# Splitting the first weights of a mixed-attention kernel on ScalarE and GpSimd instead of ScalarE and VectorE

## The chip, the cores and the metric

The kernel runs on one core of a Trainium2 chip. A core has TensorE (PE: matmuls, with PEld for its weight loads), VectorE (DVE), ScalarE (ACT) and GpSimd (POOL), and SyncE (SP), whose queue issues the kernel's DMA transfers. The metric is the device time of one execution in microseconds (us). The kernel before takes 3007.47 us, the median of three runs (2999.73 to 3012.67).

## What is computed

Two layers work on 2048 tokens of width 1024. Each layer projects its input with one wide matrix, runs four kinds of attention with four heads each (softmax with a forget gate, "fox"; stick-breaking, "sb"; low-rank latent, "mla"; attention to a memory of 256 rows, "mem"), multiplies by a gate, projects back and normalises. Cut to what matters:

```
h_res = layer_norm(x, ln_in_g, ln_in_b)
for l in range(2):
    proj = h_res @ w_in[l]
    fq, fk, fv, f_logit, sq, sk, sv, c_q, c_kv, k_rot, mq, gate = split(proj)
    out_fox = causal softmax attention(fq, fk, fv, forget(f_logit))
    out_sb = stick-breaking attention(sq, sk, sv)
    out_mla = causal softmax attention(from c_q, c_kv, k_rot)
    out_mem = softmax attention(mq, memory)
    y = (concat(out_fox, out_sb, out_mla, out_mem) * silu(gate)) @ w_out[l]
    h_res = layer_norm(alpha * h_res + y)
```

## The kernel before

All values are f32, and TensorE is fed with pairs of f16 numbers: a high half and a low half that holds what the high half left over. A product is three matmuls, high x high, high x low and low x high (`mm3`, lines 271 to 278; the three have the lines 276, 277 and 278). So each weight is read as f32 into a raw tile (pool `rawp`, 5 buffers, line 69), its largest magnitude is found on VectorE (line 128), a power of two `s` that brings it into the range of f16 is worked out (`allmax`, lines 130 to 143, two small matmuls in lines 137 and 142; `pow2`, lines 116 to 122), and then `split` (lines 145 to 147) writes the two halves: ScalarE writes `hi`, the scaled source cast to f16 (line 146), and VectorE writes `lo`, the scaled source minus `hi` (line 147).

The callers of `split` are `wprep` (line 152; the general path for weights, with loads in line 165 and splits in lines 188 and 193), `latent_w` (line 474; the weights of the latent projection: query and key latents, rotary keys and forget logits, 420 columns in all), `mla_up` and `out_proj`. In `latent_w` of the first layer the first `wprep` covers 256 columns (8 splits, each of 256 elements a partition), the second 128 columns (4 such splits), and the loop of lines 506 and 507 splits the remaining 36 columns (4 splits of 72 elements a partition). The call stands in line 1042, behind the first part of the input normalisation and ahead of the first layer.

The start of the program is thus: the input is loaded tile by tile (line 1029), normalised (`layer_norm`, lines 243 to 261: statistics on VectorE in lines 251 to 253, the square root on ScalarE in line 215, its correction on GpSimd in lines 218 to 221, the two passes of the normalisation in lines 256 and 261 on VectorE, or for every second tile in lines 258 on ScalarE and 259 on GpSimd), split into halves (`to_T`, lines 263 to 268: ScalarE in line 266, GpSimd in line 267) and turned by a DMA transpose (line 268) into `hT`. The latent projection (`latent`, lines 539 to 605) multiplies `hT` with the latent weights into a PSUM tile `pl`; for the first chunk of 512 tokens in the first layer it does so in two column ranges, 0 to 256 and 256 to 420 (line 549). The list `PLAN` (line 45) gives the order of the stages of a layer: the latents, then fox, mla, sb and mem in pairs of heads, each in four chunks of 512 tokens; the output projection (line 951) closes a layer.

The order of the instructions on each engine isn't that of the text: the program is laid out ahead of time by a scheduler that follows the order of the text as a priority and its own estimates of time (line 1083), and each engine and each DMA queue then runs its list in order.

Of the kernel before, what the change touches and what calls it, by code (L numbers as in the profile page):

```python
# [13 lines left out]
AF = mybir.ActivationFunctionType  # L14
ALU = mybir.AluOpType
# [34 lines left out]
def hybrid_kernel(ctx: ExitStack, tc: tile.TileContext, x, mem, ln_in_g, ln_in_b, mem_ln_g, mem_ln_b,  # L50
# [7 lines left out]
    def pool(name, bufs, space=None):  # L58
        if space is None:
            return ctx.enter_context(tc.tile_pool(name=name, bufs=bufs))  # L60
        return ctx.enter_context(tc.tile_pool(name=name, bufs=bufs, space=space))
# [13 lines left out]
    op = pool("op", 1)  # L75
# [8 lines left out]
    V, A, G, T = nc.vector, nc.scalar, nc.gpsimd, nc.tensor  # L84
# [57 lines left out]
        T.matmul(ps[:, P:P + n], ones_bf[0:n, :], d[0:n, 0:n], start=True, stop=True)  # L142
        return ps[:, P:P + n]

    def split(hi, lo, src, s, eng=0):
        A.activation(hi, src, AF.Copy, scale=s)
        V.scalar_tensor_tensor(lo, src, s, hi, op0=ALU.mult, op1=ALU.subtract)  # L147

# [3 lines left out]
    def wprep(groups, extra=None):  # L152
# [26 lines left out]
        for g, (srcs, dst) in enumerate(groups):  # L179
            res, s = [], ss[:, g:g + 1]  # L180
            for j in range(len(srcs)):
                if dst is None:
                    w = wp.tile([P, 2, KC, P], F16, name=nm("w"), tag="w")
                    res.append(w)
                for a in range(2):
                    rv = raws[g][2 * j + a].rearrange("p (k n) -> p k n", n=P)
                    if dst is None:
                        split(w[:, 0, a * 4:a * 4 + 4], w[:, 1, a * 4:a * 4 + 4], rv, s)
                    else:
                        his, los = dst(j, 0, a), dst(j, 1, a)  # L190
                        c = 4 // len(his)
                        for i in range(len(his)):
                            split(his[i], los[i], rv[:, i * c:(i + 1) * c], s)
            out.append((res, s, us[:, g:g + 1]))
# [105 lines left out]
    def mem_prologue():  # L300
        at = sc_at[0]
        gb, s, u = load_gb(mem_ln_g, mem_ln_b)
        sc_at[0] = at
        V.tensor_copy(mem_su[0], s)
        V.tensor_copy(mem_su[1], u)
        mt2 = ptp.tile([P, 2, KC, MEM], F16, name=nm("memT"), tag="pt")
        for t in range(2):
            xt = granule("mx")
            dma(xt, mem[t * P:(t + 1) * P])
            layer_norm([xt], gb)  # L310
            to_T(xt, mt2[:, :, :, t * P:(t + 1) * P], True)
        dma(memTd, mt2)
# [161 lines left out]
    def latent_w(l, s_h, u_h):  # L474
# [31 lines left out]
        for k in range(0, KC, 2):  # L506
            split(wl[k, 0][:, :, 384:420], wl[k, 1][:, :, 384:420], rawt[:, k:k + 2], s4)
# [12 lines left out]
    def layer(l, hT, s_h, u_h, ah, latw, norm):  # L520
# [451 lines left out]
        def start(gi):  # L972

            gens = [latent() if g == "lat" else pair(g[:-1], int(g[-1])) for g in PLAN[gi]]
            final = gi == len(PLAN) - 1
            if final:
                next(proj)
            for g in gens:
                next(g)
            return gens  # L980

        coming = start(0)
        for gi in range(len(PLAN)):
            gens, coming = coming, None
            for c in range(NCH):
                if norm:
                    next(norm, None)
                if c == AHEAD[gi] and gi + 1 < len(PLAN):
                    coming = start(gi + 1)
                for g in gens:  # L990
                    next(g)
            if gi + 1 < len(PLAN) and coming is None:
                coming = start(gi + 1)
            if l == 0 and gi == MEM_AT:
                mem_prologue()
# [41 lines left out]
    for l in range(DEPTH):  # L1037
        sc_at[0] = 32
        norm = input_norm() if l == 0 else None
        if norm:  # L1040
            next(norm)
            latw = latent_w(l, s_h, u_h)
        r = layer(l, hT, s_h, u_h, ah, latw, norm)
        if r is not None:
            hT, s_h, u_h, ah, latw = r
# [42 lines left out]
```

## Time and profile before

| | |
|---|---|
| three runs | 3012.67, 3007.47, 2999.73 us |
| profiled execution | 2999.77 us, of which the span from the first to the last instruction is 2998.0 us |
| mean granted clock of TensorE | 0.929 of full speed |
| busy: PE, DVE, ACT, POOL | 2518.7, 1979.8, 1930.7, 1530.0 us |

Busy time is the time in which an engine executes an instruction, not the time in which it waits for one. A row of a timeline gives the start in us from the span's start, the duration in us (of a run of equal instructions, from the first's start to the last's end), the engine, the line of the kernel, the operation, the tiles written and read with their shapes, and the count. Behind it stands in brackets how long the engine was idle before it, and what it waited for.

### The profile page before, as it was taken

The page shows a single profiled execution, that of the slowest core. Times are in us where ns is not written, and L with a number is a line of the kernel's source. Part 1 is how long each engine was busy: PE and PEld are TensorE (multiplying, and loading weights), DVE is VectorE, ACT ScalarE, POOL GpSimd, SP SyncE. Part 2 cuts the span into 40 slices and gives each one's busy share as a digit, 9 for nine tenths or more (in the row PEclk, how much of TensorE's full clock was granted, in tenths as well). Part 3 has the DMA queues.
Part 4 walks back from the last instruction along what each step waited for, and adds up shares of the span by engine and source line. Part 5 has one row for each costly group of instructions (what it writes and reads, how often), then busy time and mean ns, then how long its engine had stood idle before and what let it go on. Part 6 is the DMA issues. An engine that isn't in the chain of part 4 may idle for free. (4 is left out here: it accounts for less than half of the span.)

```text
span 2998.0 us, 47307 instructions
## 1 busy us (share of the span) xinstructions
PE 2518.7 (84%) x16412; PEld 1351.6 (45%) x16412; DVE 1979.8 (66%) x4313; ACT 1930.7 (64%) x3737; POOL 1530.0 (51%) x1079
## 2 busy tenths in 40 slices
PE   3689897888897876998997989888889879669998
PEld 2345454444454542543454545444445435335443
DVE  8946656876657677467545474668674776855665
ACT  3557668887777788573234566587777868776600
POOL 3415555656577889342110355355656868783300
PEclk8899999999998987999998999999999889779999
DMA  7757989998857657668744587798888576575752
GB/s 209 206 125 169 198 164 205 189 186 174 162 108 155 130 117 134 142 150 208 205 125 111 107 175 156 147 205 174 171 167 152 108 160 114 120 158 126 190 176 89
DMA packets 1225039, 469.47 MB, mean 157 GB/s; under 512 B 1040304, under 2 KB 1184944, under 8 KB 1224656
## 3 DMA queue, kind: packets, MB, share of 16 engines
q1 hardware_dynamic: 1224800, 466.46, 71.5%
q8 instruction: 128, 2.10, 0.3%
q14 instruction: 111, 0.91, 0.1%
HBM read 141.07 MB, written 50.53 MB: 64 GB/s over the span
## 5 line engine op out<-in xcount | busy, mean ns | idle before, releaser
L390 POOL TENSOR_TENSOR hl<-sb,hl 128x1024 f16<-128x1024 f32 (+7 forms) x384 | 609.0, 1597 | 648.9 <-ACT hl L389 458.6
L332 PE MATMUL s<-k,q 128*128 128x512 f16 (+3 forms) x1920 | 530.5, 376 | 210.6 <-DVE kp L405 103.9
L871 PE MATMUL o<-pt,v 128*128 128x256 f16 (+3 forms) x3456 | 403.8, 286 | 95.4 <-DMA pt<-hl 94.5
L382 ACT ACTIVATE sb<-sb,sm,sc_all 128x1024 f32<-128x1024 f32 (+7 forms) x384 | 376.4, 982 | 71.7 <-DVE sm L378 71.5
L389 ACT CAST hl<-sb 128x1024 f16<-128x1024 f32 (+7 forms) x384 | 298.3, 791 | 192.7 <-DMA pt<-hl 182.0
L871 PEld LDWEIGHTS <-v 128*64 128x64 f16 (+1 forms) x3456 | 236.4, 108 | 287.5 <-issue 148.7
L332 PEld LDWEIGHTS <-q 128*128 128x128 f16 x1920 | 182.2, 103 | 379.2 <-issue 256.8
L951 PE MATMUL s<-wo,gc 128*128 128x512 f16 x1536 | 338.0, 382 | 5.8 <-DVE yt L955 5.4
L408 POOL TENSOR_TENSOR sg<-sg,kp 128x127 f32<-128x127 f32 (+3 forms) x192 | 283.1, 1480 | 111.8 <-DVE kp L405 90.0
L415 POOL TENSOR_TENSOR hl<-sg,hl 128x128 f16<-128x128 f32 (+3 forms) x192 | 304.2, 1592 | 34.8 <-ACT hl L414 34.4
L369 DVE CUSTOM_DVE_ANT_0 sb<-s,fb 128x512 f32<-128x512 f32 (+2 forms) x320 | 183.7, 606 | 113.1 <-DMA fb<-fds 33.8
L951 PEld LDWEIGHTS <-gc 128*128 128x128 f16 x1536 | 151.2, 99 | 189.3 <-issue 12.6
L371 DVE TENSOR_SCALAR_CACHE_REDUCE sb<-s 128x512 f32<-128x512 f32 (+2 forms) x320 | 185.3, 605 | 67.7 <-POOL hl L390 37.3
L401 ACT ACTIVATE kp<-s,sc_all 128x512 f32<-128x512 f32 (+2 forms) x320 | 198.5, 631 | 41.4 <-PE s L332 28.7
L405 DVE TENSOR_TENSOR_SCAN kp<-kp,s 128x384 f32<-128x384 f32 (+7 forms) x128 | 172.4, 1348 | 79.5 <-ACT sg L402 68.3
L414 ACT CAST hl<-sg 128x128 f16<-128x128 f32 (+3 forms) x192 | 153.3, 803 | 101.1 <-DMA pt<-hl 99.3
L276 PE MATMUL pg<-hT,w 128*128 128x512 f16 x512 | 196.3, 383 | 3.7 <-DVE sb L371 1.5
L402 ACT ACTIVATE sg<-s,sc_all 128x512 f32<-128x512 f32 (+2 forms) x320 | 197.0, 632 | 2.4 <-POOL sg L408 1.8
L278 PE MATMUL pg<-hT,w 128*128 128x512 f16 x512 | 195.9, 383 | 0.3 <-DVE w L147 0.3
L277 PE MATMUL pg<-hT,w 128*128 128x512 f16 x512 | 196.1, 383 | 0.0
L276 PEld LDWEIGHTS <-w 128*128 128x128 f16 x1264 | 125.8, 100 | 149.2 <-issue 12.0
L277 PEld LDWEIGHTS <-w 128*128 128x128 f16 x1264 | 125.6, 99 | 148.0 <-issue 26.2
(238 smaller groups left out, 5712.0 us busy)
## 6 DMA issues: line engine op xcount, KB each, us to landing
raw<-in_w_in_dram SPq DMA_DIRECT2D x100, 256.0 KB, 4.7
q<-q SPq DMA_DIRECT2D x128, 128.0 KB, 2.5
fb<-fds SPq DMA_DIRECT2D x32, 512.0 KB, 4.0
gd<-gh SPq DMA_DIRECT2D x128, 128.0 KB, 2.8
raw<-in_w_out_dram SPq DMA_DIRECT2D x64, 256.0 KB, 3.3
gc<-gd SPq DMA_DIRECT2D x64, 256.0 KB, 4.1
yt<-ah SPq DMA_DIRECT2D x32, 512.0 KB, 6.6
raw<-ctd SPq DMA_DIRECT2D x48, 256.0 KB, 2.8
```

The costliest lines, as they stand in the source:

```text
L276: T.matmul(ps, lh, rh, start=(first and k == 0), stop=False)
L277: T.matmul(ps, lh, rl, start=False, stop=False)
L332: T.matmul(ps[:, :m], qs[:, h, v, j * P:(j + 1) * P], ks[c][:, h, :m], start=(v == 0), stop=last)
L382: A.activation(t, t, AF.Exp, scale=sc, bias=sm[:, j, 2:3], accum_out=su[:, b, col + j:col + j + 1])
L389: A.copy(hi, t)
L390: G.tensor_tensor(lo, t, hi, op=ALU.subtract)
L401: A.activation(keep[:, o:o + m], ps[:, :m], AF.Sigmoid, scale=nsc)
L402: A.activation(w[:, o:o + m], ps[:, :m], AF.Sigmoid, scale=sc)
L408: G.tensor_tensor(w[:, :n - 1], w[:, :n - 1], keep[:, 1:n], op=ALU.mult)
L415: G.tensor_tensor(lo, w, hi, op=ALU.subtract)
L871: T.matmul(o[r0:r1, oc + j0 * P:oc + 256], vs[k // 4][:, k % 4, h, 0:r1 - r0], pcol(pt, a, k % 8, kb, j0), start=(n == 1), stop=(n == total))
L951: T.matmul(ps, gc[a][k // 4][:, k % 4, t * P:(t + 1) * P], wo[k][:, b2, n * 512:(n + 1) * 512], start=(k == 0 and a == 0 and b2 == 0), sto ...
```

## The change

`split` gets a second form, which holds while a flag is set. The flag is set from the start of the program and is cleared in the layer function, right after the first stage of the first layer has been set up. In this form ScalarE scales the raw tile in place, ScalarE copies it into `hi` as f16, and GpSimd subtracts `hi` from the scaled tile into `lo`. VectorE has no part in it. The argument `eng`, which nothing used, is dropped.

```diff
-    def split(hi, lo, src, s, eng=0):
+    first = [True]
+
+    def split(hi, lo, src, s):
+
+        if first[0]:
+            A.activation(src, src, AF.Copy, scale=s)
+            A.copy(hi, src)
+            G.tensor_tensor(lo, src, hi, op=ALU.subtract)
+            return
         A.activation(hi, src, AF.Copy, scale=s)
         V.scalar_tensor_tensor(lo, src, s, hi, op0=ALU.mult, op1=ALU.subtract)
...
         coming = start(0)
+        first[0] = False
         for gi in range(len(PLAN)):
```

## Rows read from the trace of the kernel before

**Rows 1.** The page, part 1: busy time, share of the span, instructions.

```profile
PE 2518.7 (84%) x16412; PEld 1351.6 (45%) x16412; DVE 1979.8 (66%) x4313; ACT 1930.7 (64%) x3737; POOL 1530.0 (51%) x1079
```

**Rows 2.** Line 147, 25 to 70 us: ns min/median/max, starts, forms.

```profile
L147 DVE SCALAR_TENSOR_TENSOR w<-raw,sc_all,w x16: 290/472/2339, 28.9 to 65.0; 128x256 f16<-128x256 f32 x12, 128x72 f16<-128x72 f32 x4
```

**Rows 3.** Stretches: length, busy PE, PEld, DVE, ACT, POOL, clock, DMA.

```profile
0.00:225.00 225.00, 137.60 (x919) 82.37 (x920) 166.64 (x341) 107.78 (x217) 69.59 (x69) 0.90 0.69 180
...
75.00:90.00 15.00, 11.39 (x58) 5.76 (x56) 14.96 (x29) 8.00 (x14) 8.78 (x8) 0.89 0.49 116
```

**Rows 4.** Timeline of ScalarE: the splits' high halves, and a cast of the input.

```profile
28.31 3.30 ACT L146 ACTIVATE w<-raw,sc_all 128x256 f16<-128x256 f32 x8 [0.96 <-DVE sc_all L119]
...
38.66 1.99 ACT L266 CAST hl<-xt 128x1024 f16<-128x1024 f32 x2 [3.93 <-DVE xt L261]
...
62.08 2.68 ACT L146 ACTIVATE w<-raw,sc_all 128x256 f16<-128x256 f32 x8 [5.76 <-DVE sc_all L119]
...
97.06 2.56 ACT L146 ACTIVATE w<-raw,sc_all 128x512 f16<-128x512 f32 x4 [0.65 <-DVE sc_all L119]
```

**Rows 5.** Timeline of VectorE: the splits' low halves and steps around them.

```profile
28.86 5.17 DVE L147 SCALAR_TENSOR_TENSOR w<-raw,sc_all,w 128x256 f16<-128x256 f32 x7
33.95 1.27 DVE L251 BATCH_NORM_STATS2 bst<-xt 128x6 f32<-128x512 f32 x2
35.15 2.29 DVE L147 SCALAR_TENSOR_TENSOR w<-raw,sc_all,w 128x256 f16<-128x256 f32 x1
37.35 1.27 DVE L261 SCALAR_TENSOR_TENSOR xt<-xt,mv,gb 128x1024 f32<-128x1024 f32 x1
...
42.91 2.08 DVE L253 TENSOR_SCALAR mv<-mv 128x2 f32<-128x2 f32 x1
...
61.88 0.16 DVE L119 TENSOR_SCALAR sc_all<-pm 128x2 int32<-128x2 int32 x1 [4.70 <-PE pm L142]
...
62.77 2.48 DVE L147 SCALAR_TENSOR_TENSOR w<-raw,sc_all,w 128x256 f16<-128x256 f32 x8
...
68.64 0.69 DVE L128 TENSOR_REDUCE wm<-raw 128x1 f32<-128x512 f32 x1 [1.24 <-DMA raw<-in_w_in_dram]
...
69.31 0.16 DVE L253 TENSOR_SCALAR mv<-mv 128x2 f32<-128x2 f32 x1
```

**Rows 6.** Timeline of GpSimd beside the two batches.

```profile
32.12 0.37 POOL L221 TENSOR_TENSOR mv<-rt,ry 128x2 f32<-128x2 f32 x1
34.81 2.34 POOL L259 TENSOR_TENSOR xt<-xt,gb 128x1024 f32<-128x1024 f32 x1 [2.31 <-ACT xt L258]
39.78 5.18 POOL L267 TENSOR_TENSOR hl<-xt,hl 128x1024 f16<-128x1024 f32 x2 [2.63 <-ACT hl L266]
...
71.40 0.20 POOL L218 TENSOR_TENSOR rt<-ry,mv 128x2 f32<-128x2 f32 x1 [16.26 <-DVE ry L216]
```

**Rows 7.** GpSimd's groups by form: count, busy us, mean ns, idle.

```profile
L464 POOL TENSOR_TENSOR gh<-og,gh 128x256 f16<-128x256 f32 x128 | 90.7, 709 | 97.2 <-ACT gh L463 97.0
...
L390 POOL TENSOR_TENSOR hl<-sb,hl 128x128 f16<-128x128 f32 x32 | 15.9, 497 | 199.9 <-DVE sm L378 118.3 <-ACT hl L389 79.2 <-issue 1.5
```

**Rows 8.** Timeline of TensorE: three starts after waits.

```profile
47.66 0.40 PE L276 MATMUL pl<-w,hT 128*128 128x256 f16 x1 [6.46 <-DMA hT<-hl]
...
56.35 0.27 PE L137 MATMUL pm<-id_bf,am 128*2 128x128 bf16 x1 [4.15 <-DVE am L135]
...
64.08 0.44 PE L276 MATMUL pl<-w,hT 128*128 128x164 f16 x4 [2.23 <-ACT w L146]
```

**Rows 9.** Waits of SyncE's queue from 14 to 75 us: total, times, longest.

```profile
SPq L165 <- DVE w L147: 4.0, 3, 2.9
```

**Rows 10.** Busy time from the first scores on, first and second layer.

```profile
225.00:1345.50 1120.50, 952.38 (x6547) 522.40 (x6547) 757.59 (x1685) 847.75 (x1622) 704.24 (x487) 0.93 0.78 159
1658.80:2832.00 1173.20, 990.00 (x6795) 540.31 (x6795) 765.91 (x1669) 852.58 (x1639) 703.90 (x490) 0.92 0.73 150
```

## The prediction

> **What bounds the kernel now.** I read the page first: TensorE is busy 84% of the span, VectorE 66% [rows 1]. So over most of the span TensorE's own work and the order in which work reaches it set the time, and 1 us lost there is 1 us lost at the end. Then I looked at where the change acts. It touches 16 executions of the split, all between 28.9 and 65.0 us: 12 on pieces of 256 columns, 4 on pieces of 72 [rows 2]. The other splits of the program keep their form. In the first 225 us TensorE is busy only 137.60, so it waits for 87 us there [rows 3]. This is a start-up in which VectorE is packed for stretches (14.96 of 15 us from 75 to 90 [rows 3]), and most gaps of TensorE have a named cause. The sixteen splits come in two batches: eight from 28.31 us on, and eight (four wide, four narrow) from 62.08 us on [rows 4].
>
> What one split costs is in the timelines. ScalarE makes eight high halves in 3.30 us, 0.41 each, and the second eight in 2.68 us [rows 4]. VectorE makes seven low halves in 5.17 us, the eighth in 2.29, and the second eight in 2.48 [rows 5]: 9.94 us in all (the last row's form is that of its first piece).
>
> **The change part by part.**
>
> *What is removed.* VectorE loses those 9.94 us. In the first batch that frees it from 28.86 to 34.03 and from 35.15 to 37.4. What then stands first is the normalising step of line 261, which starts at 37.35 [rows 5] though its last input from GpSimd ended at 32.12 + 0.37 = 32.5 [rows 6]. It can come up to 4.9 us earlier, and ScalarE's cast behind it, which waited 3.93 us for it [rows 4]. In the second batch there is nothing to win: before it VectorE waits 4.70 us for TensorE, behind it 1.24 us for a load [rows 5].
>
> *What is added on ScalarE.* One more pass for each split: with the same pace, 3.30 us more in the first batch, 2.68 in the second.
>
> *What is added on GpSimd.* Twelve subtractions of 256 columns at 0.709 us (the row has the same form, f16 out of f32 and f16) are 8.5 us [rows 7]. For 72 columns there is no row: 0.37 (two columns) below [rows 6], 0.497 (128 columns) above [rows 7]; I take 0.43, so 1.7 us for four.
>
> *First batch on the path.* GpSimd gets 8 x 0.709 = 5.7 us. Between its steps there are two gaps, 2.31 us up to 34.81 and 2.63 us up to 39.78 [rows 6], 4.9 together. So 0.7 us is left over, and the two subtractions that feed the transposes (39.78, 5.18 us for both) end that much later at least. TensorE's first matmuls would now be held by the low halves up to about 41 us (32.5 + 5.7 and the step of 2.34 us at 34.81 between them), where the last of them ends at 37.4 today. This is covered: it then waits 6.46 us for the transposes at 47.66 and 4.15 us for VectorE at 56.35 [rows 8]. The 0.7 us is covered by the second wait. If the cover were gone, all 5.7 us would count (upper end); if VectorE's freed time carried the transposes forward, minus 4.9 us (lower end). I take 0, because the third tile's path goes through GpSimd, which has no time to give.
>
> By the Trainium skill, GPSIMD Engine Reference, section Engine selection, an elementwise subtraction belongs on VectorE, GpSimd being about twice as slow with two inputs. The rows give less, 0.709 us [rows 7] against a median of 0.472 [rows 2], 1.5 times; by a factor of two the eight pieces would be an estimated 7.6 us, the overflow 2.7 in place of 0.7, still covered, and the upper end 1.9 higher.
>
> *Second batch on the path.* Here TensorE waits for the weights: its matmuls of the remaining columns start at 64.08, released by ScalarE [rows 8], that is by the fifth operation of the batch (four wide, one narrow), 2.0 us after ScalarE began at 62.08 [rows 4]. With two operations for each split it is the tenth: plus 2.0 us. The low half follows 0.43 us behind on GpSimd, which has nothing else to do for 16.26 us up to 71.40 [rows 6], so its four wide pieces (2.8 us) keep pace with ScalarE's 3.4. Bounds: 0 if the narrow pieces are put first, 2.0 + 2.8 + 0.4 = 5.2 if GpSimd's pieces run only behind ScalarE's. I take 2.0: the order of the text is wide before narrow. TensorE then runs on to the end of the chunk and ScalarE waits for its result, so nothing covers this.
>
> *What is moved on the queues.* The raw tiles are given back by GpSimd instead of VectorE. SyncE's next three weight loads wait 4.0 us in total for those splits already [rows 9], and they stand ahead of other loads of the input on the same queue. They would wait about 2 us longer. The weights they bring are split at 97.06 us [rows 4], 30 us later, so I cost it at 0; without that cover it is the same 2 us over again.
>
> *Sum.* 0 + 2.0 + 0 = plus 2.0 us, between minus 4.9 and 5.7 + 5.2 = plus 10.9. The profiled execution took 2999.77 us (span 2998.0), 7.7 below the median of the three runs, 3007.47; the step is added to the median: 3009.5.
>
> **The rivals.** The measurement of this kernel can tell about 0.5%, 15 us, from no change. No direct term reaches that. What can is the order of the instructions: it isn't the order of the text (a statistics step of line 251 stands between the seventh and the eighth low half [rows 5]), but is laid out ahead by estimated times, so a shift of a few us at 30 us may put other instructions first for the rest of the program. Its price is seen between the two layers, which do the same attention work in two different surroundings. From the first scores to the output projection TensorE is idle for 1120.5 - 952.38 = 168.1 us in the first layer, and from the first scores to 2832 us, about where the second layer's output projection takes over, for 1173.2 - 990.0 = 183.2 us in the second [rows 10]: 15.1 us apart.
>
> *Slower by order.* The first layer's attention stages fall into an order as costly as the second's. Place: 225 to 1345 us; price 15.1, with the 2.0 from above 3007.5 + 17.1 = 3024.6. It decides from the first queue order that differs there. For it: TensorE's 168 us of idle time have room to grow. Against: nothing of the change acts there by itself.
>
> *Faster by order.* The second layer gets the first's idle time, minus 15.1, and the freed VectorE gives its 4.9: 2987.5. For it: 183 us of idle time, and VectorE packed in the start-up. Against: the same.
>
> *GpSimd and VectorE block each other.* VectorE's step of line 253, on two columns, takes 2.08 us from 42.91 on and ends with GpSimd's piece at 44.96 [rows 5, 6]; the same step at 69.31 takes 0.16 [rows 5]. So each new piece on GpSimd can hold VectorE. If both ends above hold together, plus 10.9: 3018.4. By the Trainium skill, SBUF — State Buffer, section Who interferes with whom, the two engines take a shared port pair as an exclusive lock for a whole instruction, which speaks against this change; the trace agrees in this row.
>
> *Nothing moves.* All is hidden behind the waits for transposes: 3007.5.
>
> **How the numbers follow.** Forecast 0.25, nothing moves 0.10, blocking 0.08: together 0.43 within 0.5%. Slower by order 0.30, a little above faster by order 0.27, since the direct term is a loss. The range goes from 2987.5 less half the spread of the shown runs (6.5), 2981, to 3007.5 + 15.1 + 10.9 = 3034. As cases of both signs hold most of the chance, the forecast's own range: 3003 to 3018.
>
> **What would show it.** In the changed profile the low halves of both batches stand on GpSimd, 16 pieces of 0.4 to 0.7 us; ScalarE's two batches take about 6.6 and 5.4 us of its time; TensorE's matmuls of 164 columns start near 66 instead of 64.08; the first scores come near 227 instead of 225; and the idle time of TensorE in the attention stages stays within some us of 168 and 183. I am wrong if the start of the first scores moves by more than 11 us, or if it doesn't and the end still moves by more than 15: then the order decided.

## The result, and the profile after

The changed kernel takes 3024.62 us (median; 3022.09 to 3038.81) beside 3007.16 for the kernel before: a ratio of 1.0066, 95% interval 1.0041 to 1.0091. It is slower by some 17 us, just beyond the 0.5% that the measurement can tell. Its profiled execution took 3028.87 us and the span is 3026.8. That execution lies above the median, and the profiled one of before lay below its own, so the 28.8 us between the two spans overstate the loss; they are used below to see places, not sizes.

First the line of the page with the busy times [rows 1]:

```profile
PE 2529.0 (84%) x16412; PEld 1359.8 (45%) x16412; DVE 1957.2 (65%) x4297; ACT 1933.7 (64%) x3753; POOL 1538.0 (51%) x1095
```

VectorE has 22.6 us less to do and TensorE, with the same 16,412 matmuls, is busy 10.3 us longer. The change did what its text says. ScalarE's timeline shows both batches of splits [rows 4] (lines from 145 on have moved by 8, those behind the layer function's loop by 9):

```profile
28.48 3.30 ACT L150 ACTIVATE raw<-raw,sc_all 128x256 f32<-128x256 f32 x8 [0.96 <-DVE sc_all L119]
31.68 0.70 ACT L151 CAST w<-raw 128x256 f16<-128x256 f32 x2
...
60.92 2.69 ACT L150 ACTIVATE raw<-raw,sc_all 128x256 f32<-128x256 f32 x8 [2.08 <-DVE sc_all L119]
63.51 0.70 ACT L151 CAST w<-raw 128x256 f16<-128x256 f32 x2
```

All the scaling passes of a batch come first, then the casts, and in each batch other passes over input tiles (line 1023, 1.15 us each) stand between the casts. GpSimd's timeline [rows 6] has the low halves:

```profile
32.15 6.15 POOL L152 TENSOR_TENSOR w<-raw,w 128x256 f16<-128x256 f32 x8
38.26 2.34 POOL L267 TENSOR_TENSOR xt<-xt,gb 128x1024 f32<-128x1024 f32 x1
...
63.98 1.30 POOL L152 TENSOR_TENSOR w<-raw,w 128x256 f16<-128x256 f32 x2 [0.45 <-ACT w L151]
...
67.04 2.15 POOL L152 TENSOR_TENSOR w<-raw,w 128x72 f16<-128x72 f32 x4
```

And TensorE's matmuls of 164 columns, which waited for the second batch [rows 8]:

```profile
66.06 0.71 PE L284 MATMUL pl<-w,hT 128*128 128x164 f16 x4 [6.75 <-ACT w L151]
67.42 0.30 PE L285 MATMUL pl<-w,hT 128*128 128x164 f16 x1 [0.65 <-POOL w L152]
```

They start at 66.06 where they started at 64.08: the 2.0 us of the prediction, though not by its working, since the batch began 1.16 us earlier (60.92 against 62.08). But the first scores, which were to follow at 227, come at 237.92 (timeline of VectorE, before and after):

```profile
225.03 0.29 DVE L369 CUSTOM_DVE_ANT_0 sb<-s,fb 128x128 f32<-128x128 f32 x1 [5.42 <-DMA fb<-fds]
```

```profile
237.92 0.29 DVE L377 CUSTOM_DVE_ANT_0 sb<-s,fb 128x128 f32<-128x128 f32 x1 [5.24 <-DMA fb<-fds]
```

**Where the 12.9 us arise.** The first scores wait for the forget gate, which needs the latents of all four chunks of rows. VectorE's timeline shows what it does with the first chunk's latents. Before:

```profile
78.08 2.10 DVE L559 TENSOR_SCALAR ss<-ss 128x4 f32<-128x4 f32 x1
...
86.74 0.88 DVE L565 SCALAR_TENSOR_TENSOR craw<-craw,ss,raw 128x256 f32<-128x256 f32 x2
```

After:

```profile
87.44 0.16 DVE L567 TENSOR_SCALAR ss<-ss 128x4 f32<-128x4 f32 x1
...
89.06 1.23 DVE L259 BATCH_NORM_STATS2 bst<-xt 128x6 f32<-128x512 f32 x2
...
94.87 1.27 DVE L264 SCALAR_TENSOR_TENSOR xt<-xt,mv,gb 128x1024 f32<-128x1024 f32 x1
...
99.50 2.89 DVE L573 SCALAR_TENSOR_TENSOR craw<-craw,ss,raw 128x256 f32<-128x256 f32 x2
...
105.50 1.48 DVE L580 TENSOR_TENSOR chl<-craw,chl 128x384 f16<-128x384 f32 x3
```

The same step is 12.8 us later (99.50 against 86.74), and between its two halves stand statistics and passes of row tiles. Their order on VectorE has changed. SyncE's queue runs in order too. Before, in its timeline:

```profile
91.34 4.44 SPq L573 DMA_TRANSPOSE cT<-chl x3
...
108.70 5.11 SPq L268 DMA_TRANSPOSE hT<-hl x2
...
135.31 1.05 SPq L1029 DMA_DIRECT2D xt<-in_x_dram x2
```

After:

```profile
106.07 5.24 SPq L581 DMA_TRANSPOSE cT<-chl x4
...
120.51 5.77 SPq L276 DMA_TRANSPOSE hT<-hl x2
...
145.58 1.52 SPq L1038 DMA_DIRECT2D xt<-in_x_dram x3
```

The queue stood before the first of these transposes; its waits from 75 to 160 us name it as the longest (total, times, longest):

```profile
SPq L581 <- DVE am L135: 17.1, 1, 17.1
```

The instruction named, of line 135, is none that a transpose needs; what ended just then is the first of the latents' low halves of line 580, begun at 105.50. Behind the queue's stop the transposes of the next rows and the loads of the last rows are 10 to 12 us late (108.70 to 120.51, 135.31 to 145.58). The statistics of the last row tile start at 155.1 instead of 143.4 (the line's summary, first and last start behind the durations; before, then after):

```profile
L251 DVE BATCH_NORM_STATS2 bst<-xt x32: 627/676/695, 7.8 to 143.4; 128x6 f32<-128x512 f32 x32
```

```profile
L259 DVE BATCH_NORM_STATS2 bst<-xt x32: 637/676/695, 7.9 to 155.1; 128x6 f32<-128x512 f32 x32
```

From there the delay of 11.7 us runs on, a little longer, to the first scores.

**Where the rest arises.** Of the 28.8 us between the two spans, 18.5 are more idle time of TensorE and 10.3 are longer busy time of the same matmuls. Busy times of the start-up and of the two layers' attention stages, as in [rows 3, 10]:

```profile
0.00:237.90 237.90, 149.67 (x996) 90.16 (x997) 150.61 (x326) 113.10 (x235) 76.44 (x85) 0.89 0.66 170
237.90:1371.00 1133.10, 953.58 (x6470) 520.33 (x6470) 759.59 (x1684) 846.33 (x1621) 703.22 (x487) 0.92 0.77 157
1683.00:2860.80 1177.80, 987.75 (x6796) 543.02 (x6796) 757.96 (x1670) 851.56 (x1639) 704.72 (x490) 0.93 0.74 150
```

Up to the first scores TensorE idles 237.9 - 149.67 = 88.2 us, as before (87.4): it did 77 more matmuls there (996 against 919). So the late start is work pulled ahead, and it should have come back later. It didn't. In the first layer's attention stages TensorE has 77 matmuls fewer to do (6470 against 6547), yet it idles 1133.1 - 953.58 = 179.5 us in place of 168.1, and in the second layer 190.0 in place of 183.2. One execution against another of the same order differs by some 5 us here: e1, the kernel before in its own order, idles 164.1 us in the first layer, and e4, the changed kernel again, 184.6.

### The profile page after: what moved, and what is told of

It is laid out like the page before. It is cut to its first block, busy times and chain, and to the rows that moved or that the text cites. A ratio compares the mean times of both kernels' runs of the same rounds, so it can differ in the third digit from the quotient of the medians.

```text
span 3026.8 us, 47324 instructions
## 1 busy us (share of the span) xinstructions
PE 2529.0 (84%) x16412; PEld 1359.8 (45%) x16412; DVE 1957.2 (65%) x4297; ACT 1933.7 (64%) x3753; POOL 1538.0 (51%) x1095
## 5 line engine op out<-in xcount | busy, mean ns | idle before, releaser
L377 DVE CUSTOM_DVE_ANT_0 sb<-s,fb 128x512 f32<-128x512 f32 (+2 forms) x320 | 184.2, 606 | 131.8 <-DMA fb<-fds 56.0
```

## The experiments

The question is whether the loss comes from the sixteen splits or from the order of all other work. The program is laid out by a scheduler, and one changed duration can reorder it. SyncE's list, to which the change itself adds nothing, differs between the two traces from its 17th instruction on, and 7% of its pairs of neighbours aren't neighbours any more (VectorE's 15%, ScalarE's 14%, GpSimd's 10%, TensorE's 2.5%, counted by line, operation, tiles and shape). To separate the two, an order is written down for each engine and queue and forced by dependencies that only order instructions of one engine and carry no wait:

```diff
+    for e, p in _old_order().items():
...
+        for a, b in zip(line, line[1:]):
+            tc.add_manual_dep(b, a.name, info, reason="old order")
```

All ratios are to the kernel before, run beside it.

**e1: the kernel before in its own forced order.** The edit is the one above, alone.

> The kernel before, with the instruction order of every engine and queue written down and forced (the same order as it had). Control: both theories expect the ratio 1.000 within 0.2%, first scores at 225 us.

Measured: 3006.33 us, ratio 1.0001 (0.9989 to 1.0013), first scores at 224.7. Forcing an order costs nothing that can be seen, here to within 0.12%.

**e2: the new splits in the old order.**

```diff
+            a = A.activation(src, src, AF.Copy, scale=s)
+            c = A.copy(hi, src)
+            g = G.tensor_tensor(lo, src, hi, op=ALU.subtract)
...
+    pin(tc, nc, {"DVE": [m[0] for m in marks]},
...
```

`pin` forces the old order with VectorE's sixteen low halves taken out; the new ScalarE pieces stand in the place of the old ones, GpSimd's behind the nearest step of its list (the first eight behind line 221's second step, the other eight behind the pair of line 267).

> The change's 16 splits (ScalarE twice, GpSimd), but every other instruction of the program forced into the order it had before. Order theory (the loss comes from the new order of the whole program): ratio 1.000 to 1.0015, that is 0 to 5 us, first scores at 225 to 229 us, the second batch's matmuls at about 66. Direct theory (the loss comes from the sixteen splits themselves, GpSimd and ScalarE being slower or in the way): 1.005 to 1.008, first scores at about 238 us.

Measured: 3008.26 us, ratio 1.0005 (0.9994 to 1.0015), first scores at 226.7. ScalarE's and TensorE's timelines at the second batch, and the busy times up to the first layer's output projection:

```profile
61.34 0.51 ACT L153 ACTIVATE raw<-raw,sc_all 128x256 f32<-128x256 f32 x1 [4.84 <-DVE sc_all L119]
```

```profile
65.42 0.71 PE L288 MATMUL pl<-w,hT 128*128 128x164 f16 x4 [4.31 <-ACT w L154]
```

```profile
226.70:1344.50 1117.80, 950.80 (x6546) 521.77 (x6545) 758.86 (x1685) 847.38 (x1622) 704.77 (x487) 0.93 0.79 159
```

The idle time there is 167.0 us, as in the kernel before. By the medians the splits in the old order cost 1.9 us over e1, which agrees with the sum's 2.0; the intervals would allow nothing, or some 5 us. What goes beyond that needs another order.

**e3 and e5: the old splits in the new order.** VectorE's sixteen low halves are put back, each batch right behind the last step that works out its scale, and all else is forced into the changed kernel's order. It was run twice, the second time beside the changed kernel.

```diff
-            A.activation(src, src, AF.Copy, scale=s)
-            A.copy(hi, src)
-            G.tensor_tensor(lo, src, hi, op=ALU.subtract)
+        A.activation(hi, src, AF.Copy, scale=s)
+        v = V.scalar_tensor_tensor(lo, src, s, hi, op0=ALU.mult, op1=ALU.subtract)
...
+    pin(tc, nc, {"Activation": [m[0] for m in marks], "Pool": [m[1] for m in marks]},
...
```

> The old splits (ScalarE once, VectorE), but every other instruction forced into the order of the changed kernel. Order theory: 1.004 to 1.008, first scores at 235 to 238 us, though no split is changed. Direct theory: 0.999 to 1.001, first scores at about 225 us.

> The old splits in the changed kernel's order, once more beside the changed kernel itself. Theory: again near 1.0033, first scores at 237, so that its distance to the changed kernel is the part that needs both the new splits and the new order. Rival: level with the changed kernel within 0.1%, and then the order is all of the loss.

Measured: 3015.11 us, ratio 1.0033 (1.0020 to 1.0046), and 3016.62 us, 1.0037 (1.0023 to 1.0050). The first scores come at 237.2 and 235.9, though no split was changed. In e3 the stretches up to them and up to the output projection read

```profile
0.00:237.20 237.20, 152.71 (x996) 91.06 (x997) 159.33 (x342) 109.37 (x219) 67.47 (x69) 0.88 0.67 171
237.20:1364.10 1126.90, 950.38 (x6470) 517.69 (x6470) 760.14 (x1684) 847.80 (x1620) 704.18 (x487) 0.92 0.78 158
```

so 176.5 us idle in the attention stages. The order alone brings the late first scores, most of the added idle time, and half of the loss.

**e4 and e8: the changed kernel again, free and forced.** e4 is the changed kernel without an edit, e8 has the edit of e1 with the changed kernel's own lists, so that it differs from e3 by the splits alone.

> The changed kernel once more, on the same chip as the next three. Theory (the new order costs about 10 us, and the new splits with it another 10): ratio to before 1.005 to 1.008, first scores at 238, above the old splits in the new order by 0.2% or more. Rival (order alone, and the rest was chance of which executions were timed): ratio 1.003 to 1.0045, level with the old splits in the new order.

> The changed kernel, its own order of every engine and queue written down and forced, as the old splits were forced into it before. Theory (new splits and new order together cost what neither costs alone): ratio 1.005 to 1.009, as the changed kernel itself. Rival (the forcing takes time away by itself in this order, and the two kernels with the old splits were faster for that): ratio 1.002 to 1.005.

Measured: 1.0073 (1.0055 to 1.0091) and 1.0067 (1.0050 to 1.0083). Both rivals fall: the loss repeats, and the forcing takes no time away. In this order the new splits cost 3028.03 - 3016.62 = 11 us (e4 over e5, run side by side), and 3026.51 - 3016.62 = 10 us by e8, where they cost 2 in the old one. By the spread of the runs each of these is an estimate to within some 5 us. What the splits do at the start doesn't depend on the execution: TensorE's matmuls of 164 columns start 2.00 us behind ScalarE's first operation of the second batch with the old splits (62.70 against 60.70 in e3), and 5.14 us with the new ones in the changed kernel's order (65.82 against 60.68 in e8):

```profile
62.70 0.44 PE L282 MATMUL pl<-w,hT 128*128 128x164 f16 x4 [2.66 <-ACT w L150]
```

```profile
65.82 0.70 PE L284 MATMUL pl<-w,hT 128*128 128x164 f16 x4 [6.93 <-ACT w L151]
```

**e7: first the latents, then the rows.** The changed kernel's order with one block moved: VectorE and ScalarE do three of the first chunk's four latent tiles ahead of the row tiles (17 and 3 instructions). The edit is in the forced lists alone; otherwise the kernel is e8.

> The changed kernel in its own order on every engine and queue, but for one block: VectorE and ScalarE finish the first chunk's latents (17 instructions on VectorE, 3 on ScalarE) ahead of the normalisation of the row tiles that the new order had put between. Theory (SP's queue stands 17 us at that chunk's transposes, and the transposes and row loads behind them come late): the first transposes of the latents leave at 93 to 98 in place of 106, the wait on SP shrinks to 4 to 9 us, first scores come at 226 to 234 in place of 238, and the time falls by 4 to 12 us against the changed kernel. Rival (the row tiles themselves are the limit, and now wait for the latents on VectorE): the first scores stay within 2 us of 238 and the time does too.

Measured: 1.0066 (1.0046 to 1.0086), level with the changed kernel; first scores at 237.49, last row statistics at 155.0. SyncE's and ScalarE's timelines:

```profile
92.34 20.04 SPq L581 DMA_TRANSPOSE cT<-chl x4
```

```profile
108.75 0.54 ACT L579 CAST chl<-craw 128x384 f16<-128x384 f32 x1
```

The first transpose left at 92.34, about as expected, but the fourth tile's cast had kept its place on ScalarE, at 108.75, and the queue stood for it instead: 20.04 us from the first of the four to the last. The rows behind gained nothing. The edit was too small to tell whether the queue or VectorE's time is the limit; it shows that moving one block on two engines doesn't undo the order of the rest.

**e6: the new splits, only the start-up in the old order.** The forced part ends at the first scores; the scheduler lays out the rest.

```diff
-        for a, b in zip(line, line[1:]):
-            tc.add_manual_dep(b, a.name, info, reason="old order")
+        n, last = {"Pool": 69, "SP": 124, "DVE": 341, "Activation": 181, "PE": 913}[e], 0
...
+        for at in range(1, len(line)):
+            tc.add_manual_dep(line[at], line[min(at - 1, last)].name, info, reason="old order")
```

> The change's sixteen splits, the order of before forced on every engine and queue only as far as the first scores, and everything later left to the scheduler. As built, what the scheduler then makes of it keeps the order of before through the first layer and departs from it only in the second. Theory (the start-up's order is what costs): first scores at 226 to 228, ratio 0.999 to 1.002. Rival (the later order loses on its own account): first scores at 226 to 228 all the same, but the ratio over 1.003.

What stands there of the first layer is not exact: TensorE's list departs from the old one at its 2841st matmul of 16,412, in the first layer's mla stage. Measured: 2993.46 us, ratio 0.9964 (0.9950 to 0.9978), first scores at 226.2. Neither theory expected a gain. This is a third order, and it is faster than the kernel before although its splits are the new ones.

**e9: the old splits in that third order.** The edit is that of e1 with the lists that the scheduler made for e6.

> The old splits, everything in the order that the scheduler made once the start-up was forced (the third order, in which the new splits measured 0.9964). Theory (the order is what pays, and the new splits cost 1.5 to 2 us of direct work): ratio 0.994 to 0.997, not slower than 0.9964 by more than 0.1%, first scores at 224 to 226. Rival (the gain needs the new splits): ratio 0.999 to 1.001.

Measured: 2986.30 us, ratio 0.9927 (0.9911 to 0.9943): faster than both kernels, by 21 and 38 us, with exactly the instructions of the kernel before. Its page has

```profile
PE 2514.4 (84%) x16412; PEld 1352.0 (45%) x16412; DVE 1967.3 (66%) x4313; ACT 1930.4 (65%) x3737; POOL 1531.1 (51%) x1079
```

In a span of 2979.2 TensorE idles 464.8 us where the kernel before had 479.3, and most of that lies in the second layer's attention stages (172.2 us of idle time up to its output projection, where the kernel before had 182.8 and e10, below, 175.8). There the score matmuls of the kernel before twice wait long for VectorE's scans, 7.7 us up to 2394.9 and 9.1 up to 2582.5; in e9 the longest such wait is 5.0 us. The gain was expected to be at most 0.6%; it is larger, since here too the new splits cost more than 2 us (0.9964 against 0.9927, 11 us).

**e10: another order by priority.** The kernel before with a higher priority for loading and normalising the incoming rows; no split changed, nothing forced.

```diff
+            with tc.high_priority(offset=400):
                 for t2 in range(2 * c, 2 * c + 2):
```

> The kernel before with no split changed: only the loading and normalising of the incoming rows is given a higher priority in the scheduler, so that it makes another order of the same instructions. Theory (any new order of this program moves the time by some tenths of a per cent, either way): ratio off 1 by 0.2 to 0.8%, the sign open; if the last row tile's statistics start before 143 us, first scores before 225. Rival (the scheduler's orders are all alike, and the changed kernel's was a rare bad one): ratio within 0.15% of 1.

Measured: 2999.63 us, ratio 0.9969 (0.9954 to 0.9983), with the first scores as late as in the changed kernel:

```profile
237.16 0.29 DVE L369 CUSTOM_DVE_ANT_0 sb<-s,fb 128x128 f32<-128x128 f32 x1 [5.36 <-DMA fb<-fds]
```

**e11: the first eight splits alone.**

```diff
+        first.append(0)
-        if first[0]:
+        if first[0] and len(first) <= 9:
```

> Only the first eight splits in the new form, the other eight as before, the order left to the scheduler. Theory (the order decides, not the number of pieces): whatever its ratio is, it goes with the start of the first scores, and it need not lie between 1 and the changed kernel's 1.007: 0.996 to 1.008. Rival (each new split costs its own share): ratio 1.002 to 1.005, first scores 4 to 8 us late.

Measured: 3031.49 us, ratio 1.0078 (1.0061 to 1.0096). Half of the change costs no less than all of it, and the first scores are early here (225.91). The loss lies behind them, in the stages of the first layer (fox; mla; sb with mem):

```profile
225.90:544.30 318.40, 274.44 (x2029) 155.53 (x2029) 202.68 (x608) 223.61 (x398) 165.82 (x116) 0.95 0.86 177
544.30:833.80 289.50, 249.60 (x1648) 133.34 (x1647) 211.99 (x614) 229.28 (x408) 172.87 (x120) 0.96 0.89 177
833.80:1370.00 536.20, 435.88 (x2931) 237.73 (x2929) 351.24 (x467) 392.61 (x817) 363.69 (x254) 0.90 0.63 130
```

TensorE idles 1144.1 - 959.92 = 184.2 us there, where the kernel before has 168.1. The traces name two of the waits, in the sb stage. Score matmuls wait twice for VectorE, longer than the longest such waits of that stage in the kernel before (first e11, then before):

```profile
1125.93 1.01 PE L341 MATMUL s<-k,q 128*128 128x512 f16 x2 [10.27 <-DVE wt L125]
1145.85 1.49 PE L341 MATMUL s<-k,q 128*128 128x512 f16 x3 [9.68 <-DVE wt L179]
```

```profile
1110.17 2.50 PE L332 MATMUL s<-k,q 128*128 128x512 f16 x6 [5.01 <-DVE kp L405]
1128.62 1.04 PE L332 MATMUL s<-k,q 128*128 128x512 f16 x2 [6.21 <-DVE kp L405]
```

In e11 four low halves of later weights (6.97 us from 1112.55 on) and four largest-magnitude passes stand in VectorE's list between two scans of the sb stage (line 414, line 405 before: a cumulative product along a row); in the kernel before three low halves and one such pass stand between two scans there. The instructions named in e11 are none that a score matmul needs; two scans end just then (1125.88 and 1145.80). So one place where the order acts is where the preparation of later weights falls among the steps that TensorE waits for.

In e10 and e11 the rivals fall: a new order moves the time either way, and the time doesn't go with the number of new splits. But the first theory's half sentence, that the time goes with the start of the first scores, falls as well: late first scores came with a gain, early ones with a loss.

**e12: ScalarE's half alone, in the new order.** The raw weights are scaled in place and cast, and VectorE subtracts.

```diff
+            A.activation(src, src, AF.Copy, scale=s)
+            A.copy(hi, src)
+            v = V.tensor_tensor(lo, src, hi, op=ALU.subtract)
```

> ScalarE's half of the change alone, in the changed kernel's order: the sixteen raw weights are scaled in place and cast by two ScalarE instructions, but VectorE subtracts as before (a plain subtraction, without the scale) and GpSimd does nothing for it. Theory (handing the low halves to GpSimd is what costs the last third of a per cent in this order): ratio 1.002 to 1.005, level with the old splits in that order, first scores at 236 to 238. Rival (ScalarE's second pass over the pieces, a delay of about 2 us ahead of the first matmuls, is enough in this order): ratio 1.006 to 1.008, level with the changed kernel.

Measured: 3021.32 us, ratio 1.0051 (1.0032 to 1.0069), first scores at 239.3: between the two theories, and its interval touches both. Inconclusive.

All of it by order and form of the splits:

| order | old splits | new splits |
|---|---|---|
| of the kernel before | 1.0001 (e1) | 1.0005 (e2) |
| of the changed kernel | 1.0033, 1.0037 (e3, e5) | 1.0066, 1.0073, 1.0067 (the change, e4, e8) |
| third | 0.9927 (e9) | 0.9964 (e6) |

## Why the prediction was right and wrong

The measured 3024.62 us lies in the wide range (2981 to 3034) and outside the forecast's own (3003 to 3018). The forecast, 3009.5, and the two other cases within 0.5%, which together had a chance of 0.43, aren't what came. What came is "slower by order", priced at 3024.6.

*The direct terms were right, in the order they were worked out for.* The second batch was costed at plus 2.0, ten operations in place of five ahead of the matmuls. In e2 these start 4.08 us behind ScalarE's first operation (65.42 against 61.34), where it was 2.00 before: as costed. In the changed kernel it is 5.14, since all eight scalings stand ahead of the casts and another pass between the casts; there the term was 3.1 and not 2.0, and that the start moved by 2.0 all the same is luck. The whole of e2 is 1.9 us over e1 by the medians (each with an interval of some 3 us to either side). The first batch was costed at 0, and so it was in e2: the step behind the second wait, TensorE's matmul of line 137, comes at 56.54 where it comes at 56.26 in e1. VectorE's step was to come up to 4.9 us earlier; in e2 and in the changed kernel it came 5.3 us earlier (32.09 and 32.10) and bought nothing in e2, as the text argued. GpSimd's pieces of 256 columns took 0.67 each where nothing stood beside them, a little less than the 0.709 of the row. By the Trainium skill's factor of two [GPSIMD Engine Reference, section Engine selection] they would have taken an estimated 0.94, and the trace doesn't show it.

*Blocking is there, and was covered.* The first eight pieces took 8.02 us in e2, where three of them took 1.65 or 1.66 beside VectorE's passes, and 6.15 in the changed kernel, where only the first met one. Line summaries of these eight (shortest, median and longest in ns), e2 and the changed kernel:

```profile
L155 POOL TENSOR_TENSOR w<-raw,w x8: 666/673/1658, 32.0 to 39.4; 128x256 f16<-128x256 f32 x8
```

```profile
L152 POOL TENSOR_TENSOR w<-raw,w x8: 664/666/1760, 32.1 to 37.6; 128x256 f16<-128x256 f32 x8
```

VectorE's pair of line 573 took 2.89 us at 99.50 in the changed kernel instead of 0.88, beside a GpSimd pass of 2.53 us from 99.18 on. It agrees with the rule that the Trainium skill gives [SBUF — State Buffer, section Who interferes with whom], that the port pair which the two engines share is an exclusive lock. As a cause of the loss in the old order it falls: e2 has the blocking and not the loss.

*The step that failed* is the one behind the chances: "nothing of the change acts there by itself" was set against the order rival and kept it at 0.30, while sixteen changed splits from 28 us on changed the lists of all engines. The prediction had seen that the program is laid out ahead by estimated times, and treated a new order as possible. Yet it counted a new order that costs as much as the old one among the likely cases. The runs show no such order: the three that the scheduler made freely (the change, e10, e11) and the one that followed a forced start (e9, with the old splits) moved the time by 0.3 to 0.8%, in the change and in e11 with the new splits' share in it. With that, "same" deserved far less, and the two order rivals more, in about equal parts.

*The price came out by luck, and the place half right.* "The first layer's attention stages fall into an order as costly as the second's" put 15.1 us on the order and 2.0 on the splits. Added to the median of before they give the measured time to a tenth, but each of the two terms is off: the order alone cost 7.5 and 10.8 us (e3 and e5), and the splits in that order about as much again. The idle time was to grow from 168.1 to 183.2 in the first layer; it grew to 179.5 (e8: 181.0). TensorE's longer busy time, 10.3 us of the 28.8 between the spans, was not in the sum at all. Not foreseen was the start-up either: the prediction's own condition "I am wrong if the start of the first scores moves by more than 11 us" came true with 12.9. But it was a poor sign. Those 12.9 us hold 77 matmuls done ahead of time, e10 has the same delay with only 10 matmuls more (929 against 919) and gains 0.3%, while e11 has none and loses 0.8%.

*"Faster by order"* named minus 15.1 and 4.9. The third order shows that such orders exist (minus 21 us in e9); that this change would find one was chance.

*What stays open.* The same sixteen splits cost 2 us in one order and some 10 in two others. Why, the traces don't settle. In e8 against e3 (13.9 us between the spans) 10.5 us arise in the second layer's attention stages; in e4 against e5 (12.9 us), the same two kernels but for the forcing, 5.0 arise in the first layer's and 3.4 in the second's. So no one place and no one wait carries it, and e12 couldn't divide it between ScalarE's second pass and GpSimd. That a shift of 2 to 3 us at the start meets other transfers later, and that tight orders have less slack to take it up, would fit, but is only argued.

## What to carry to other kernels

Where a scheduler lays out the program, an edit of a few instructions has two prices: its own, here 2 us in the old order and some 10 in two others, and that of the new order, here between 21 us less and 11 us more. Price the two apart by forcing the old order around the new instructions before you keep or reject an edit, and don't read a change of under 1% in a free layout as the edit's own: in this kernel it was in part a draw among orders. The reverse pays too: the best kernel of this study is the old one in an order that came up by chance.

## What was not expected of the hardware

- TensorE did 77 matmuls more ahead of the first scores in the new order, and the stage behind them didn't get shorter. The kernel before does 1970 matmuls in its first fox stage, in 303.8 us, 265.96 of them busy at a granted clock of 0.96. In the new order 1868 are left, and the stage took 301.9 to 304.7 us, 258.9 to 262.3 of them busy at 0.93 or 0.94 (e3, e4, e5, e8), and 309.6 us with 267.74 busy at 0.91 in the profiled execution of the change, an execution that e4, the same kernel, did not repeat.
- In the changed kernel a VectorE pass of 256 columns, 0.48 us before, took 2.50 us beside a GpSimd pass of 2.53: a single pass of the neighbour held a short VectorE instruction for several times its own length. In e2 it went the other way, GpSimd's pieces taking 1.65 us in place of 0.67 beside VectorE's passes.
